# Retention outputs of one layer: PE's order set to transposes, preceding tile's outputs, gate products, scores, with q, k, v in a tile of their own

## The chip, the core and the metric

The kernel is one launch on one NeuronCore of a Trainium2 chip. The metric is the device time of that launch in microseconds (us), as the median of several runs. Five engines work beside each other, each through its own queue in order: PE (TensorE, the matrix engine), DVE (VectorE), ACT (ScalarE), POOL (GpSimd) and SP (SyncE, which here only issues DMAs).

## The reference

One layer of a hybrid backbone on 1024 tokens of width 1024 with 256 context tokens, in float32: modulated RMSNorm, one input projection, differential attention beside bidirectional retention, an output projection, then a routed mixture of 64 experts. The change lies in the retention, which in the reference reads (both directions; for a chunk of 128 tokens):

```
scores = einsum('bnihd,bnjhd->bnhij', qc, kc) * decay
intra  = einsum('bnhij,bnjhe->bnihe', scores, vc)
cross  = einsum('bnihd,nbhde->bnihe', q_dec, state_prev)
out    = intra + cross
r      = silu(gate) * rmsnorm(out, ret_norm_g)
```

Here `qc`, `kc` are 4 heads of 64, `vc` 4 heads of 128, `gate` is 512 columns of the input projection, and `state_prev` is the running sum of decayed k-v products that reaches the chunk.

## The kernel before, in words

The kernel runs stage after stage: column modulation, a projection of retention's q and k, the k-v products and states, **the retention outputs**, then queries, keys, values, attention, output projection, experts. Tiles are 128 tokens, so there are 8 of them, `t` = 0 to 7. A scheduler takes the program as written and puts each engine's instructions into a fixed order before the launch, by its own estimate of when each is ready; on the chip each engine then follows its list, waiting on semaphores. So the order of one engine can hold pieces of several tiles mixed, and a late instruction holds back everything behind it on its engine.

The retention outputs (lines 538 to 584) go through `t` from 7 down to 0. For one tile:

- `load_qkv` (L538) fetches q and k as `rqk` (L540) and v as `vt` (L542) from DRAM, where earlier stages stored them. It is called one tile ahead. Both tiles come from a ring of 10 buffers of 2 KB per partition, named `g2`, which all the small tiles of the stage share.
- `state_step` (L496 to L500) brings the backward state one tile further: DVE multiplies by the decay (`sst`, L499) and adds (`ST`, L500).
- `project` (L225) makes the gate: 24 products of 128x512 on PE (L228, tile `pp`: 8 slices of the width, each three times for a split of float32 in a high and a low part). ACT takes Silu of it (`gt`, L553) and POOL multiplies by the norm's weights (L554).
- PE transposes q and k (L555, recorded under the helper's line L392, `p<-cst,rqk`), and ACT copies them out (`qkT`, L557).
- DVE makes q with decay (`qd`, L559), PE transposes it (L561, again L392, `p<-cst,qd`), ACT copies it out (`qdT`, L563).
- PE makes the scores (`pss`, L567), DVE multiplies by the decay matrix `Dm` (`sT`, L569).
- PE makes the output (`po`): per head one product with v (L572) and one with the state (L573).
- ACT squares and sums the four heads (`sqs`, L577). `rstd_cols` (L154) takes the root: one operation on DVE (`rs_v`, L157) and one on POOL (`rs_r`, L159). DVE scales and gates the output (`r_o`, L581), SP stores it (L582).

Between these, `ada_rest` (L401) spreads other work over the stage: DMAs of 256 KB (`ada_l`, L408, two buffers) and one DVE operation on each (`ada_a`, L410 and L412); every eighth step, `ada_row` (L417) adds a product of one row on PE (`par`, L420) and a DVE operation on it (`ada_r`, L424 and L428). At the end of the stage `load_chunk` (L202) splits the next stage's weights: ACT makes the high part (`whi`, L209), DVE the low part (`wlo`, L210).

Of the kernel before, what the change touches and what calls it, by code (L numbers as in the profile page):

```python
# [9 lines left out]
F32 = mybir.dt.float32  # L10
# [4 lines left out]
AF = mybir.ActivationFunctionType  # L15
OP = mybir.AluOpType
# [4 lines left out]
P = 128  # L21
# [63 lines left out]
def hybrid_layer_kernel(ctx: ExitStack, tc: tile.TileContext, A, out, dbg=None):  # L85
    nc = tc.nc
    pe, dve, act, pool, sp = nc.tensor, nc.vector, nc.scalar, nc.gpsimd, nc.sync
# [90 lines left out]
    hv = ctx.enter_context(tc.tile_pool(name="hv", bufs=1, side="left"))  # L178
# [67 lines left out]
    NG2 = 10  # L246
# [9 lines left out]
    rng = wk.tile([P, P], F32, name="rng")  # L256
# [144 lines left out]
    def ada_rest(count):  # L401

        for n, k in ada_left[:count]:
            if k == 0:
                ada_acc[n] = wk.tile([P, 512], F32, name="ada_a", tag="ada_a", bufs=2)
            ac = ada_acc[n]
            aw = wk.tile([P, 512], F32, name="ada_l", tag="ada_l", bufs=2)
            sp.dma_start(aw, ada[:, k, 2048 + 512 * n:2560 + 512 * n])  # L408
            if k == 0:
                dve.tensor_scalar(ac, aw, cc[:, 0, 0:1], None, op0=OP.mult)  # L410
            else:
                dve.scalar_tensor_tensor(ac, aw, cc[:, k, 0:1], ac, op0=OP.mult, op1=OP.add)  # L412
            if k == 2 and n > 0:
                ada_row(n - 1)
        del ada_left[:count]

    def ada_row(n):  # L417
        c0 = 2048 + 512 * n
        pr_ = psa.tile([1, 512], F32, name="par", tag="po", bufs=2)
        pe.matmul(pr_, ones[:, 0:1], ada_acc.pop(n), start=True, stop=True)  # L420
        rw = wk.tile([1, 512], F32, name="ada_r", tag="ada_r")
        bw = wk.tile([1, 512], F32, name="ada_b", tag="ada_b")
        sp.dma_start(bw, A["ada_b"][:, c0:c0 + 512])
        dve.tensor_add(rw, pr_, bw)  # L424
        if n // 2 == 2:
            gw = wk.tile([1, 512], F32, name="ada_g", tag="ada_b")
            sp.dma_start(gw, A["norm2_g"][:, (n % 2) * 512:(n % 2 + 1) * 512])
            dve.scalar_tensor_tensor(rw, rw, 1.0, gw, op0=OP.add, op1=OP.mult)  # L428
        sp.dma_start(rows_d[n // 2:n // 2 + 1, (n % 2) * 512:(n % 2 + 1) * 512], rw)
# [5 lines left out]
    W = [], []  # L435
# [9 lines left out]
    for i, g in enumerate(pairs):  # L445
        for t in (2 * g - 2, 2 * g - 1):
            if t < 0:
                ps = project(t, W, 256, 512)
# [15 lines left out]
    Dm = wk.tile([P, H, P], F32, name="Dm")  # L464
# [26 lines left out]
    W = load_chunk(2048)  # L491
    ST = [s4.tile([P, 2, H, P], F32, name="ST") for _ in range(4)]
    ST = [ST[t // 2][:, t % 2] for t in range(NT)]
    GSb = GS[:, :, None].to_broadcast([P, H, P])

    def state_step(dst, src, kvp, half):  # L496
        s = slice(64 * half, 64 * half + 64)
        tmp = wk.tile([P, H, P], F32, name="sst", tag="g2", bufs=NG2)
        dve.tensor_tensor(tmp[s], src[s], GSb[s], op=OP.mult)  # L499
        dve.tensor_add(dst[s], tmp[s], kvp[s])  # L500

    kvc0 = None
    for t in range(-2, NT):
        ada_rest(VADA)
        ps = project(t, W)
# [13 lines left out]
        for h in range(H):  # L519
            pe.matmul(pk[:, h, :], kd[:, h].rearrange("p a b -> p (a b)"), v[:, h * P:(h + 1) * P],  # L520
                      start=True, stop=True)
# [13 lines left out]

    W = load_chunk(2560)

    def load_qkv(t):  # L538
        qk = wk.tile([P, 512], F32, name="rqk", tag="g2", bufs=NG2)
        sp.dma_start(qk, rqk_d[t * P:(t + 1) * P])  # L540
        vt = wk.tile([P, 512], F32, name="vt", tag="g2", bufs=NG2)
        sp.dma_start(vt, rv_d[t * P:(t + 1) * P])  # L542
        return qk, vt

    qkv = {NT - 1: load_qkv(NT - 1)}
    for t in reversed(range(NT)):
        qk, vt = qkv.pop(t)
        if t > 0:
            qkv[t - 1] = load_qkv(t - 1)
            state_step(ST[t - 1], ST[t], ST[t - 1], 1)  # L550
        ps = project(t, W)
        gt = wk.tile([P, H, P], F32, name="gt", tag="g2", bufs=NG2)
        act.activation(gt.rearrange("p h e -> p (h e)"), ps, AF.Silu)  # L553
        pool.tensor_tensor(gt, gt, rng[:, None, :].to_broadcast([P, H, P]), op=OP.mult)  # L554
        pt = transpose4(qk, "tp")  # L555
        qkT = wk.tile([P, 4, P], F32, name="qkT", tag="g2", bufs=NG2)
        act.activation(qkT, pt, AF.Copy)  # L557
        qd = wk.tile([P, H, 2, 64], F32, name="qd", tag="g2", bufs=NG2)
        dve.tensor_tensor(qd, qk[:, 0:256].rearrange("p (h d) -> p h d", h=H)[:, :, None, :].to_broadcast([P, H, 2, 64]),  # L559
                          Wd[:, 0, :, :, None].to_broadcast([P, H, 2, 64]), op=OP.mult)  # L560
        pt = transpose4(qd.rearrange("p h a d -> p (h a d)"), "tp")  # L561
        qdT = wk.tile([P, H, P], F32, name="qdT", tag="g2", bufs=NG2)
        act.activation(qdT, pt, AF.Copy)  # L563
        pss = psa.tile([P, 2, 4, P], F32, name="pss", tag="ps", bufs=1)
        for h in range(H):
            s = slice(64 * (h % 2), 64 * (h % 2) + 64)
            pe.matmul(pss[:, h % 2, h // 2, :], qkT[s, 2 + h // 2, :], qkT[s, h // 2, :], start=True, stop=True)  # L567
        sT = wk.tile([P, H, P], F32, name="sT", tag="g2", bufs=NG2)
        dve.tensor_tensor(sT.rearrange("p (a b) j -> p a b j", a=2), pss[:, :, 0:2, :], Dm.rearrange("p (a b) j -> p a b j", a=2), op=OP.mult)  # L569
        po_ = psa.tile([P, H, P], F32, name="po", tag="po", bufs=2)  # L570
        for h in range(H):
            pe.matmul(po_[:, h, :], sT[:, 2 * (h % 2) + h // 2, :], vt[:, h * P:(h + 1) * P], start=True, stop=False)  # L572
            pe.matmul(po_[:, h, :], qdT[:, h, :], ST[t][:, h, :], start=False, stop=True)  # L573
        ssq = wk.tile([P, 4], F32, name="ssq4", tag="ssq4", bufs=2)
        sqs = wk.tile([P, P], F32, name="sqs", tag="sqs", bufs=2)
        for h in range(H):
            act.activation(sqs, po_[:, h, :], AF.Square, accum_out=ssq[:, h:h + 1])  # L577
        rs = rstd_cols(wk, ssq, P, 4, 1.0 / P)
        r = wk.tile([P, H, P], F32, name="r_o", tag="g2", bufs=NG2)
        for h in range(H):  # L580
            dve.scalar_tensor_tensor(r[:, h, :], po_[:, h, :], rs[:, h:h + 1], gt[:, h, :], op0=OP.mult, op1=OP.mult)  # L581
        sp.dma_start(mix_d[t * P:(t + 1) * P, 512:1024], r.rearrange("p h e -> p (h e)"))  # L582
        ada_rest(GADA)
    ada_row(NT - 1)

    wk_ctx.close()
    NG2 = 4
    wq_ctx = ExitStack()
    wk = open_pool(wq_ctx, "wq", "right")
# [5 lines left out]
    W = load_chunk(0)  # L595
    for t in range(NT):
        o = apply_rope(wk, project(t, W), t, NG2)
        pt = transpose4(o, "tp")
        qs = wqs.tile([P, 4, 4, P], F32R, name="qs", tag="qs", bufs=2)
        for m in range(2):  # L600
            a, b = slice(64 * m, 64 * m + 64), slice(64 * (1 - m), 64 * (1 - m) + 64)
# [19 lines left out]
    W = load_chunk(512)  # L621
    for t in range(-2, NT):
        ps = project(t, W)
# [5 lines left out]
        pt = transpose4(o, "tp")  # L629
        c = slice((t + 2) * P, (t + 3) * P)  # L630
        for m in range(2):
            a, b = slice(64 * m, 64 * m + 64), slice(64 * (1 - m), 64 * (1 - m) + 64)
# [4 lines left out]
    W = load_chunk(1024)  # L637
# [20 lines left out]
    vt = [2 * g + j - 2 for g in (*LZ, 1, 4) for j in range(2)]  # L658
# [825 lines left out]
    with tc.For_i(0, n_over, 1) as j:  # L1484
        e = sp.value_load(olist[0:1, 0, bass.ds(j, 1)], min_val=0, max_val=NEXP - 1)
# [14 lines left out]
        for q in range(2):  # L1500
            pt = bank("tr", [P, 4, P])
# [5 lines left out]
        for i in range(2):  # L1507
            for k in range(KT):
                pe.matmul(pu[:, i * 256:(i + 1) * 256], xT[:, k, :], w13[:, i, k, :], start=(k == 0),
                          stop=(k == KT - 1))  # L1510
# [65 lines left out]
```

## Time and profile before

| what | value |
|---|---|
| median of 3 runs | 1822.42 us (1821.26 to 1834.03) |
| the profiled execution | 1815.02 us, its span 1813.2 us |
| mean granted TensorE clock | 0.968 of full |
| PE, DVE, ACT, POOL busy | 92%, 75%, 53%, 30% of the span |
| retention outputs | from about 180 to 284 us of the span |

The profile is of one execution. A row of a timeline gives the start, how long the instruction took, the engine, the line, what is written and read, and, in brackets, how long the engine had been idle before it and whose result it waited for. Durations of PE's products are modelled at their ends, so that neighbours overlap: spacing of starts says more than the duration. [...]

### The profile page before, as it was taken

The page shows a single profiled execution, that of the slowest core. Times are in us where ns is not written, and L with a number is a line of the kernel's source. Part 1 is how long each engine was busy: PE and PEld are TensorE (multiplying, and loading weights), DVE is VectorE, ACT ScalarE, POOL GpSimd, SP SyncE. Part 2 cuts the span into 40 slices and gives each one's busy share as a digit, 9 for nine tenths or more (in the row PEclk, how much of TensorE's full clock was granted, in tenths as well). Part 3 has the DMA queues.
Part 4 walks back from the last instruction along what each step waited for, and adds up shares of the span by engine and source line. Part 5 has one row for each costly group of instructions (what it writes and reads, how often), then busy time and mean ns, then how long its engine had stood idle before and what let it go on. Part 6 is the DMA issues. An engine that isn't in the chain of part 4 may idle for free.

```text
span 1813.2 us, 23071 instructions
## 1 busy us (share of the span) xinstructions
PE 1672.5 (92%) x8022; PEld 1273.8 (70%) x8022; DVE 1355.0 (75%) x2080; ACT 960.0 (53%) x1537; POOL 536.5 (30%) x384
## 2 busy tenths in 40 slices
PE   5899889999899989888899999999999999999992
PEld 3687667778666658666687777777777777777771
DVE  7866566651778766786577899888988989878873
ACT  6632223322578752232356787666765665566652
POOL 0100113200221130436434444343445343332331
PEclk9999989999899999998899999999999999999996
DMA  9675545801211144232989999999999999999976
GB/s 316 205 216 181 177 137 120 180 0 59 71 41 59 35 174 164 94 117 41 281 233 310 324 326 327 319 316 314 321 320 330 353 333 357 315 305 315 314 222 212
DMA packets 128413, 400.57 MB, mean 221 GB/s; under 512 B 13110, under 2 KB 49654, under 8 KB 103336
## 3 DMA queue, kind: packets, MB, share of 16 engines
q1 hardware_dynamic: 81000, 297.10, 45.8%
q0 software_dynamic: 46144, 97.80, 23.0%
q10 hardware_dynamic: 1152, 4.19, 0.6%
q8 instruction: 64, 1.05, 0.2%
q14 instruction: 53, 0.43, 0.1%
HBM read 324.45 MB, written 74.60 MB: 220 GB/s over the span
## 4 chain that ended last, share of the span: by engine, by line
PE 56%; DVE 15%; DMA 13%; ACT 7%; issue 5%; POOL 2%; another core or an unknown queue 1%; SPq 1%; POOLq 0%; ACTq 0%; DVEq 0%
PE up L1230 20%; PE py L1230 9%; PE pp L228 7%; DMA acc<-y,sidx 6%; PE tr L1214 3%; PE py L97 3%; PE pp L97 3%; DMA eraw<-in_exp_w_dram 3%; PE pS L97 3%; DVE w L1160 2%; ACT w L1159 2%; PE pu L97 2%; DVE nmx L729 2%; PE ptt L97 1%
## 5 line engine op out<-in xcount | busy, mean ns | idle before, releaser
L1230 PE MATMUL up<-w,xT 128*128 128x512 f32 (+1 forms) x2136 | 533.6, 399 | 4.7 <-DVE xT L1219 4.2
L1160 DVE TENSOR_TENSOR w<-eraw,w 128x1024 fp32r<-128x1024 f32 x390 | 459.8, 1217 | 43.3 <-ACT w L1159 41.9
L1159 ACT ACTIVATE w<-eraw 128x1024 fp32r<-128x1024 f32 x390 | 399.6, 1056 | 110.4 <-PE up L1230 59.1
L1230 PEld LDWEIGHTS up<-w,xT 128*128 128x128 f32 (+1 forms) x2136 | 384.5, 184 | 102.6 <-DVE xT L1219 7.8
L1169 POOL DMA_INDIRECT acc<-y,sidx x96 | 203.1, 2116 | 477.4 <-DMA acc<-y,sidx 215.6
L1230 PE MATMUL py<-w,ehT 128*128 128x512 f32 (+1 forms) x1116 | 293.6, 405 | 1.9 <-DVE ehT L1219 1.9
L1230 PEld LDWEIGHTS py<-w,ehT 128*128 128x128 f32 (+1 forms) x1116 | 198.2, 185 | 49.3 <-DVE ehT L1219 2.5
L1281 DVE SCALAR_TENSOR_TENSOR y<-py,swt,g2r 128x512 f32<-128x512 f32 (+2 forms) x192 | 137.9, 740 | 57.5 <-DMA acc<-y,sidx 38.7
L1198 POOL DMA_INDIRECT xg<-h2tab,sidx x96 | 132.8, 1384 | 68.5 <-PE tr L1214 43.6
L228 PE MATMUL pp<-whi,hTh 128*128 128x512 f32 (+1 forms) x368 | 148.0, 403 | 1.4 <-ACT hTh L386 1.2
L228 PE MATMUL pp<-wlo,hTh 128*128 128x512 f32 (+1 forms) x368 | 147.7, 403 | 0.0
L729 DVE TENSOR_REDUCE nmx<-pS 128x1 f32<-128x1280 f32 x64 | 95.1, 1487 | 67.2 <-PE pS L97 67.0
L1256 ACT ACTIVATE sl<-up 128x256 f32<-128x256 f32 (+1 forms) x104 | 39.7, 382 | 151.5 <-PE up L1230 139.9
L1219 DVE TENSOR_TENSOR xT<-tr,xT 128x512 fp32r<-128x512 f32 (+1 forms) x167 | 104.3, 655 | 14.9 <-ACT xT L1218 14.4
L159 POOL TENSOR_TENSOR rs_r<-rs_v,mhalf 128x1 f32<-128x1 f32 (+1 forms) x34 | 28.2, 830 | 268.3 <-DVE rs_v L157 166.7
L1018 POOL DMA_INDIRECT slots<-dat,ad x64 | 68.6, 1072 | 109.8 <-DVE dat L1015 54.9
L97 PE MATMUL pS<-K,qsl 128*128 128x512 f32 x336 | 94.7, 419 | 2.8 <-ACT an L737 1.9
L1258 DVE TENSOR_TENSOR hn<-up,sl 128x256 f32<-128x256 f32 (+1 forms) x104 | 64.8, 623 | 43.0 <-ACT sl L1256 42.0
L1218 ACT ACTIVATE xT<-tr 128x512 fp32r<-128x512 f32 (+1 forms) x167 | 89.1, 571 | 12.7 <-PE tr L1214 6.3
L1214 PEld LDWEIGHTS tr<-cst,xg 128*128 128x128 f32 (+2 forms) x800 | 79.0, 140 | 22.0 <-issue 7.1
L97 PE MATMUL py<-wo,mT 128*128 128x512 f32 x384 | 90.7, 393 | 0.0
L1214 PE MATMUL tr<-cst,xg 128*128 128x128 f32 (+2 forms) x800 | 90.3, 253 | 0.0
(324 smaller groups left out, 2503.7 us busy)
## 6 DMA issues: line engine op xcount, KB each, us to landing
eraw<-in_exp_w_dram SPq DMA_DIRECT2D x192, 1024.0 KB
ada_l<-in_ada_w_dram SPq DMA_DIRECT2D x64, 256.0 KB
wraw<-in_w_in_dram SPq DMA_DIRECT2D x24, 512.0 KB
aw<-in_ada_w_dram SPq DMA_DIRECT2D x8, 1024.0 KB
qsp<-qs POOLq DMA_DIRECT2D x32, 256.0 KB
qsl<-qsp POOLq DMA_DIRECT2D x7, 1024.0 KB
xt<-in_x_dram SPq DMA_DIRECT2D x8, 512.0 KB
wor<-in_w_out_dram SPq DMA_DIRECT2D x8, 512.0 KB
```

Of the source, the lines that this page charges most:

```text
L97: i = getattr(self.eng, name)(*args, **kw)
L228: pe.matmul(kw["out"], kw["lhsT"], kw["rhs"], start=kw["start"], stop=kw["stop"])
L729: dve.tensor_reduce(self.nmx, self.pS, axis=AX.X, op=OP.max, negate=True)
L1159: act.activation(hi, raw, AF.Copy)
L1160: dve.tensor_sub(lo, raw, hi.bitcast(F32))
L1169: x = pool.indirect_dma_start(out=acc, out_offset=bass.IndirectOffsetOnAxis(ap=idx, axis=0), in_=y, in_offset=None, compute_op=OP.add)
L1198: self.load = pool.indirect_dma_start(out=self.xg[:self.n], out_offset=None, in_=h2tab, in_offset=bass.IndirectOffsetOnAxis(ap=self.idx, a ...
L1214: pe.transpose(pt[:, i, :], src[:rows, k * P:(k + 1) * P], ident[:rows, :rows])
L1218: act.activation(hi, pt, AF.Copy)
L1219: dve.tensor_sub(lo, pt, hi.bitcast(F32))
L1230: pe.matmul(po, ops[o][:, k, :], w(k), start=(k == 0 and j == 0), stop=(k == nk - 1 and j == len(seq) - 1))
L1281: dve.scalar_tensor_tensor(y[:n, c], ps[i][:n], self.wt, g2r[:n, c], op0=OP.mult, op1=OP.mult)
```

## The change

The tile's work is written in another order, in a software pipeline of one tile. A tile's two sets of transposes come first, then the outputs of the preceding tile (`ret_out`, now a function), the state step and the loads for the next tile, the gate's products, the scores with `sT`. `qd` is now made in `load_qkv`, a tile ahead. q, k and v go into one tile `rows_qv` with two places (`t % 2`), in a buffer outside the ring (`hv0`, free in this stage). The last tile's outputs stand behind the loop. No arithmetic changes. (Numbers of lines below 544 move little; the lines of the kernel after are 9 higher from the next stage on.)

```diff
+    rows_qv = hv.tile([P, 2, 2, 512], F32, name="rows_qv", tag="hv0")
+
     def load_qkv(t):
-        qk = wk.tile([P, 512], F32, name="rqk", tag="g2", bufs=NG2)
+        qk, vt = rows_qv[:, t % 2, 0], rows_qv[:, t % 2, 1]
         sp.dma_start(qk, rqk_d[t * P:(t + 1) * P])
-        vt = wk.tile([P, 512], F32, name="vt", tag="g2", bufs=NG2)
         sp.dma_start(vt, rv_d[t * P:(t + 1) * P])
-        return qk, vt
+        qd = ...
+        dve.tensor_tensor(qd, ...)
+        return qk, vt, qd
+
+    def ret_out(t, sT, qdT, vt, gt):
+        ...
-    qkv = {NT - 1: load_qkv(NT - 1)}
-    for t in reversed(range(NT)):
-        ...
+    nxt, out_args = load_qkv(NT - 1), None
+    for t in reversed(range(NT)):
+        qk, vt, qd = nxt
+        pt = transpose4(qk, "tp")
+        ...
+        pt = transpose4(qd.rearrange("p h a d -> p (h a d)"), "tp")
+        ...
+        if out_args:
+            ret_out(*out_args)
+        if t > 0:
+            state_step(ST[t - 1], ST[t], ST[t - 1], 1)
+            nxt = load_qkv(t - 1)
+        ps = project(t, W)
+        ...
+        out_args = t, sT, qdT, vt, gt
         ada_rest(GADA)
+    ret_out(*out_args)
     ada_row(NT - 1)
```

PE before, around the outputs of tile 5 (`pss_1911`, `qd_1902` and `po_1918` are tile 5's, `pp_1978` is tile 4's gate; the number behind a name is the buffer's):

```order
L228 MATMUL pp_1978<-whi_1623,hTh3_674 128x512
L567 MATMUL pss_1911<-qkT_1900 128x128 x3
L392 MATMUL p4_1904<-cst_60,qd_1902 128x128 x4
L567 MATMUL pss_1911<-qkT_1900 128x128
L228 MATMUL pp_1978<-wlo_1624,hTh3_674 128x512
L228 MATMUL pp_1978<-whi_1623,hTlz_549 128x512
L228 MATMUL pp_1978<-whi_1629,hTh3_674 128x512
L228 MATMUL pp_1978<-wlo_1630,hTh3_674 128x512
L572 MATMUL po_1918<-vt_1760,sT_1916 128x128
```

Ahead of the outputs stand four products of the next tile's gate, behind the transposes of the tile's own `qd`. PE after, around the outputs of the same tile (`pss_1906`, `sT_1911` and `po_1955` are tile 5's, `p4_1941`, `qd_1876` and `pp_1987` tile 4's):

```order
L228 MATMUL pp_1878<-whi_1641,hTlz_549 128x512
L587 MATMUL pss_1906<-qkT_1837 128x128 x4
L420 MATMUL par_1916<-ada_a_1712,ones_63 1x512
L392 MATMUL p4_1941<-cst_60,rows_qv_1645 128x128 x4
L392 MATMUL p4_1948<-cst_60,qd_1876 128x128 x4
L554 MATMUL po_1955<-rows_qv_1645,sT_1911 128x128
```

Before, a tile's transposes of `qd`, its scores and its outputs stand a few gate products apart; after, the scores, the next tile's transposes and the outputs stand together, and 24 gate products in one piece follow.

DVE before, from the gating of tile 6 to the scores of tile 5:

```order
L157 TENSOR_SCALAR rs_v_1831<-ssq4_1825 128x4
L581 SCALAR_TENSOR_TENSOR r_o_1835<-po_1816,rs_r_1833,gt_1790 128x128 x4
L499 TENSOR_TENSOR sst_1864<-ST_1102,GS_138 64x512
L412 SCALAR_TENSOR_TENSOR ada_a_1853<-ada_l_1959,cc_99,ada_a_1853 128x512
L500 TENSOR_TENSOR ST_1102<-sst_1864,ST_1102 64x512
L559 TENSOR_TENSOR qd_1902<-rqk_1758,Wd_129 128x512
L412 SCALAR_TENSOR_TENSOR ada_a_1853<-ada_l_1962,cc_99,ada_a_1853 128x512
L569 TENSOR_TENSOR sT_1916<-pss_1911,Dm_1034 128x512
```

The tile's own `qd` and one `ada_a` stand ahead of its `sT`. DVE after, the same stretch (`qd_1876` is tile 4's):

```order
L157 TENSOR_SCALAR rs_v_1861<-ssq4_1855 128x4
L563 SCALAR_TENSOR_TENSOR r_o_1865<-po_1846,rs_r_1863,gt_1803 128x128 x4
L499 TENSOR_TENSOR sst_1871<-ST_1102,GS_138 64x512
L547 TENSOR_TENSOR qd_1876<-rows_qv_1645,Wd_129 128x512
L500 TENSOR_TENSOR ST_1102<-sst_1871,ST_1102 64x512
L412 SCALAR_TENSOR_TENSOR ada_a_1825<-ada_l_1935,cc_99,ada_a_1825 128x512
L412 SCALAR_TENSOR_TENSOR ada_a_1825<-ada_l_1938,cc_99,ada_a_1825 128x512
L589 TENSOR_TENSOR sT_1911<-pss_1906,Dm_1034 128x512
```

`qd` moved from the tile to the one ahead of it; the gating of tile 6 stands ahead of the scores of tile 5 in both.

## Rows read from the trace of the kernel before

**Rows 1.** The page's head and its first part: busy time, share of the span and instructions of each engine.

```profile
span 1813.2 us, 23071 instructions
PE 1672.5 (92%) x8022; PEld 1273.8 (70%) x8022; DVE 1355.0 (75%) x2080; ACT 960.0 (53%) x1537; POOL 536.5 (30%) x384
```

**Rows 2.** The view of windows: a stretch, its length, busy time of PE, of PE's weight loads, DVE, ACT and POOL with their counts, then the granted clock, the DMA share and GB/s.

```profile
175.00:190.00 15.00, 15.00 (x86) 12.31 (x85) 9.54 (x13) 6.75 (x9) 1.29 (x1) 1.00 0.91 307
190.00:205.00 15.00, 13.47 (x65) 10.12 (x65) 8.49 (x15) 4.62 (x19) 2.68 (x3) 0.89 0.49 149
220.00:235.00 15.00, 12.97 (x56) 9.80 (x55) 8.62 (x14) 3.16 (x11) 1.98 (x2) 0.77 0.36 114
280.00:295.00 15.00, 15.00 (x73) 11.72 (x72) 6.86 (x16) 3.83 (x13) 1.01 (x1) 1.00 0.05 19
...
188.15:190.13 1.98, 1.98 (x17) 1.86 (x16) 0.00 (x0) 0.00 (x0) 0.00 (x0) 1.00 0.92 347
228.85:232.28 3.43, 3.43 (x17) 3.31 (x15) 0.37 (x1) 0.00 (x0) 0.00 (x0) 0.53 0.52 153
258.29:260.07 1.78, 1.78 (x18) 1.78 (x16) 0.74 (x2) 0.00 (x0) 0.00 (x0) 1.00 0.56 157
...
188.15:280.70 92.55, 80.89 (x403) 62.54 (x403) 57.11 (x95) 25.97 (x81) 17.75 (x14) 0.89 0.47 148
```

**Rows 3.** The view of waits from 170 to 300 us: who waited for whom, us in total, times, the longest.

```profile
PE p L392 <- DVE qd L559: 11.7, 7, 2.3
```

**Rows 4.** The chain of work that ended last, in order of time: start, us, what.

```profile
143.32 5.36 PE pp L228 x23
...
183.35 0.44 PE p L392 x4
...
186.55 0.65 PE pss L567 x8
...
190.20 0.96 PE par L420 x2
...
192.18 1.09 POOL rs_r L159
```

**Rows 5.** The timeline of PE: start, us, engine, line, what, count, idle before.

```profile
163.85 1.13 PE L520 MATMUL pk<-rv,kd 128*128 128x128 f32 x8 [0.56 <-DVE kd L516]
...
188.15 0.49 PE L572 MATMUL po<-vt,sT 128*128 128x128 f32 x2
...
196.99 0.66 PE L392 MATMUL p<-cst,qd 128*128 128x128 f32 x4 [1.53 <-DVE qd L559]
...
210.77 0.66 PE L392 MATMUL p<-cst,qd 128*128 128x128 f32 x4 [2.28 <-DVE qd L559]
...
256.16 0.66 PE L392 MATMUL p<-cst,qd 128*128 128x128 f32 x4 [1.09 <-DVE qd L559]
...
280.70 0.38 PE L572 MATMUL po<-vt,sT 128*128 128x128 f32 x2
```

**Rows 6.** The timeline of DVE, columns as in rows 5.

```profile
175.61 2.35 DVE L210 TENSOR_TENSOR wlo<-wraw,whi 128x1024 fp32r<-128x1024 f32 x2
...
186.74 0.75 DVE L412 SCALAR_TENSOR_TENSOR ada_a<-ada_l,cc,ada_a 128x512 f32<-128x512 f32 x1 [3.07 <-DMA ada_l<-in_ada_w_dram]
187.41 0.68 DVE L569 TENSOR_TENSOR sT<-pss,Dm 128x512 f32<-128x512 f32 x1
...
194.46 1.75 DVE L499 TENSOR_TENSOR sst<-ST,GS 64x512 f32<-64x512 f32 x1
196.24 0.69 DVE L559 TENSOR_TENSOR qd<-rqk,Wd 128x512 f32<-128x512 f32 x1
196.97 0.69 DVE L500 TENSOR_TENSOR ST<-sst,ST 64x512 f32<-64x512 f32 x1
...
205.75 1.13 DVE L581 SCALAR_TENSOR_TENSOR r_o<-po,rs_r,gt 128x128 f32<-128x128 f32 x4 [1.19 <-POOL rs_r L159]
206.91 0.69 DVE L499 TENSOR_TENSOR sst<-ST,GS 64x512 f32<-64x512 f32 x1
207.63 1.65 DVE L412 SCALAR_TENSOR_TENSOR ada_a<-ada_l,cc,ada_a 128x512 f32<-128x512 f32 x1
...
277.40 1.13 DVE L581 SCALAR_TENSOR_TENSOR r_o<-po,rs_r,gt 128x128 f32<-128x128 f32 x4 [1.19 <-POOL rs_r L159]
```

**Rows 7.** The timelines of ACT and POOL, columns as in rows 5.

```profile
190.24 0.28 ACT L577 ACTIVATE sqs<-po 128x128 f32<-128x128 f32 x1 [3.06 <-PE po L573]
...
202.79 0.28 ACT L577 ACTIVATE sqs<-po 128x128 f32<-128x128 f32 x1 [4.46 <-PE po L573]
...
194.38 1.27 POOL L554 TENSOR_TENSOR gt<-gt,rng 128x512 f32<-128x512 f32 x1 [1.12 <-ACT gt L553]
...
207.19 1.53 POOL L554 TENSOR_TENSOR gt<-gt,rng 128x512 f32<-128x512 f32 x1 [1.48 <-ACT gt L553]
...
277.33 1.27 POOL L554 TENSOR_TENSOR gt<-gt,rng 128x512 f32<-128x512 f32 x1
```

More of the change, by code (lines that the diff above doesn't have):

```diff
@@ L536, in hybrid_layer_kernel @@
     W = load_chunk(2560)
+    rows_qv = hv.tile([P, 2, 2, 512], F32, name="rows_qv", tag="hv0")
     def load_qkv(t):
-        qk = wk.tile([P, 512], F32, name="rqk", tag="g2", bufs=NG2)
+        qk, vt = rows_qv[:, t % 2, 0], rows_qv[:, t % 2, 1]
         sp.dma_start(qk, rqk_d[t * P:(t + 1) * P])
-        vt = wk.tile([P, 512], F32, name="vt", tag="g2", bufs=NG2)
         sp.dma_start(vt, rv_d[t * P:(t + 1) * P])
-        return qk, vt
-    qkv = {NT - 1: load_qkv(NT - 1)}
-    for t in reversed(range(NT)):
[L547 to L557, printed above, removed]
         qd = wk.tile([P, H, 2, 64], F32, name="qd", tag="g2", bufs=NG2)
@@ L560, in hybrid_layer_kernel @@
                           Wd[:, 0, :, :, None].to_broadcast([P, H, 2, 64]), op=OP.mult)
[L561 to L569, printed above, removed]
+        return qk, vt, qd
+    def ret_out(t, sT, qdT, vt, gt):
         po_ = psa.tile([P, H, P], F32, name="po", tag="po", bufs=2)
@@ L582, in hybrid_layer_kernel @@
         sp.dma_start(mix_d[t * P:(t + 1) * P, 512:1024], r.rearrange("p h e -> p (h e)"))
+    nxt, out_args = load_qkv(NT - 1), None
+    for t in reversed(range(NT)):
+        qk, vt, qd = nxt
+        pt = transpose4(qk, "tp")
+        qkT = wk.tile([P, 4, P], F32, name="qkT", tag="g2", bufs=NG2)
+        act.activation(qkT, pt, AF.Copy)
+        pt = transpose4(qd.rearrange("p h a d -> p (h a d)"), "tp")
+        qdT = wk.tile([P, H, P], F32, name="qdT", tag="g2", bufs=NG2)
+        act.activation(qdT, pt, AF.Copy)
+        if out_args:
[4 more added lines that the diff above has]
+        ps = project(t, W)
+        gt = wk.tile([P, H, P], F32, name="gt", tag="g2", bufs=NG2)
+        act.activation(gt.rearrange("p h e -> p (h e)"), ps, AF.Silu)
+        pool.tensor_tensor(gt, gt, rng[:, None, :].to_broadcast([P, H, P]), op=OP.mult)
+        pss = psa.tile([P, 2, 4, P], F32, name="pss", tag="ps", bufs=1)
+        for h in range(H):
+            s = slice(64 * (h % 2), 64 * (h % 2) + 64)
+            pe.matmul(pss[:, h % 2, h // 2, :], qkT[s, 2 + h // 2, :], qkT[s, h // 2, :], start=True, stop=True)
+        sT = wk.tile([P, H, P], F32, name="sT", tag="g2", bufs=NG2)
+        dve.tensor_tensor(sT.rearrange("p (a b) j -> p a b j", a=2), pss[:, :, 0:2, :], Dm.rearrange("p (a b) j -> p a b j", a=2), op=OP.mult)
+        out_args = t, sT, qdT, vt, gt
         ada_rest(GADA)
+    ret_out(*out_args)
     ada_row(NT - 1)
```

## The prediction

> **What bounds the kernel now.** I read the page's busy shares first, then the windows over the stage, then who waited for whom, then the timelines of PE and DVE. PE is busy 92% of the span [rows 1], so a gain must come from places where it is not. The windows show one: from 175 to 190 us and from 280 to 295 PE is busy all the time at full clock, but between them it stands at 13.0 to 13.5 of 15 us, and the granted clock sinks to 0.77 in the worst stretch [rows 2]. That is the stage that is changed. From the first output of tile 7 at 188.15 to that of tile 0 at 280.70 there are seven gaps in 92.55 us, 13.2 us each [rows 2, 5].
>
> The waits name the reason: seven times PE waited for `qd`, 11.7 us together [rows 3]. [...]
>
> **What PE needs at least.** In the new order a gap holds 24 gate products at 5.36/23 = 0.233 us, so 5.6; scores 0.65; two sets of transposes at 0.44; outputs 1.98; together 9.1 us, and with `par` (0.96) 10.1 us, which stands in three of the seven gaps [rows 2, 4]. The transposes no longer wait: `qd` of a tile is made before the scores of the tile ahead of it, so the 11.7 us of waits on it go.
>
> **What is late next.** The change moves PE's list, but DVE's list keeps one thing: the gating `r_o` of a tile stands ahead of the scores `sT` of the next, and the outputs of the next tile need that `sT`. So a chain runs from output to output, through DVE, and I add it up:
>
> - outputs to the first square on ACT, 188.15 to 190.24: 2.09 [rows 5, 7]
> - first square to `r_o`, through ACT, DVE and POOL's root, 202.79 to 205.75: 2.96 [rows 6, 7]
> - `r_o` to `sst`, 205.75 to 206.91: 1.16; `sst` to the next, 0.72; `qd` 0.73; `ST` 0.72 like `sst` [rows 6]
> - two `ada_a` at a spacing of 0.67 (186.74 to 187.41): 1.34 [rows 6]
> - `sT` and the handover to PE, 187.41 to 188.15: 0.74 [rows 5, 6]
>
> The sum is 10.46 us. That is above PE's 9.1 and, by 0.4, above its 10.1. So PE will wait ahead of the outputs instead of ahead of the transposes of `qd`: shorter by some 3 us per gap than today's 13.2, if nothing is added. Two things are.
>
> First, POOL's `gt` follows the gate's products by ACT's Silu, and so falls beside `ST` and the two `ada_a`. Beside `gt`, `sst` took 1.75 instead of 0.69 us and an `ada_a` 1.65 instead of 0.75, and they ended only after POOL had; `r_o`, which reads `po` from PSUM, ran its 1.13 us beside `gt` unchanged [rows 6, 7]. I take 1.0 us per gap, between 0 (a `gt` that comes late meets nothing) and 1.06. What `gt` does to `sT`, no row shows; its operands are like those of `r_o` (one from PSUM), so I take 0, with the same bounds. [...]
>
> Second, a wait of 2 us or more ahead of the outputs brings the clock down, and the outputs are in the chain. They cost 1.45 more when all of them run at the lower level, 0 when the fall comes behind them. I take 0.5, near the 0 end, because in the gaps of before the lower level covered all of them only once [rows 2].
>
> **The sum.** A gap of 10.46 + 1.0 + 0.5 = 12.0 us. Five gaps (7 to 2) are like that: 60.0, plus 0.67 for an `ada_a` that the order puts into the `r_o` of tile 3: 60.7. The gap 2 to 1 has no `ada_a` left and `gt` meets only `sT`: 10.46 - 1.34 + 0.5 = 9.6. In the gap 1 to 0 the splits of the next weights, three `wlo`, stand between `r_o` and `sT`: 2.35 us for two [rows 6], so 3.5 for three; 2.09 + 2.96 + 1.16 + 3.5 + 0.74 + 1.0 + 0.5 = 12.0. Together 82.3, against 92.55: 10.2 us less.
>
> The ends: the `ada_a` ahead of tile 7's `sT` waited 3.07 us for its DMA [rows 6]. In SP's new order two of the four loads that stood ahead of that DMA are issued earlier. I take 1.0 us of gain, between 0 and the 3.07. Against that, the new PE order has 11 products fewer done when the last outputs begin (15 products of the queries' first tile stood ahead of the stage's last `par` before, 4 do now): 11 x 0.233 = 2.6 us to be done later. And behind the last outputs the clock is likely down, after the three `wlo`: 1.2 us, between 0 and 1.45. Behind the stage I count nothing: PE is busy all the time there [rows 2], so what is won is passed on, and the stages after are not touched.
>
> Net: 10.2 + 1.0 - 2.6 - 1.2 = 7.4 us. The profiled execution, 1813.2 us of span and 1.8 us around it, would take 1815.0 - 7.4 = 1807.6. The median of the runs, 1822.4, lies 7.4 us above that execution; the stage is the same in all, so I take the same us from it: 1822.4 - 7.4 = 1815.0 us, 0.4% less.
>
> **Edits that I cost at nothing.** The place for q, k, v outside the ring of ten: with two places, the load for tile t-2 must wait until tile t's outputs have read v. It stands in SP's queue ahead of the `ada_l` loads of the next gap, so these leave some 2.1 us into the gap and are wanted at 8.4 (2.09 + 2.96 + 1.16 + 0.72 + 0.73 + 0.72); 6.3 us of room cover twice the longest wait for such a load in the rows, 3.07 [rows 6]. If the cover is gone, a gap grows by what is late of it, since both `ada_a` stand in the chain. The store of `r_o`, too, holds SP; behind it stand only loads that are wanted after `sT`. ACT and POOL do the same work; ACT's evictions lie beside 24 gate products.
>
> **Rivals.**
>
> A. *The chain through DVE is not late, PE alone sets the gap.* For it: 24 products in one piece, and PE the busiest engine. Against it: the order, in which `sT` of a tile stands behind `r_o` of the tile before. Four gaps of 9.1 and three of 10.1 make 66.7, 25.9 less; 25.9 + 1.0 - 2.6 = 24.3 us: 1798 us.
>
> B. *The clock takes it all back, the kernel gets slower.* The wait now stands in one piece right ahead of the outputs, and the outputs are the first link of the chain. From a wait of 1.5 us on, the trace shows the fall. If it comes in every gap and covers the outputs, and the rest runs at the 0.77 of the stretch 220 to 235 [rows 2], the chain is 10.46 + 1.06 + 1.45 = 13.0 and PE's work 10.1/0.77 = 13.1: three gaps of 13.1, two of 13.0 with 0.67 more, 9.1/0.77 = 11.8 for the gap 2 to 1, and 13.0 make 90.8. That saves 1.8, and 2.6 + 1.45 go at the end: 2.3 us slower, 1824.7. Against it: after 1.09 us there was no fall, and gaps with `par` leave PE a wait of no more than 2 us. [...]
>
> C. *The loads are late* and the `ada_a` wait in each of the five gaps as the worst did, 3.07 us: 15 us given back on the forecast, 1830. Against it is the room worked out above.
>
> **How the numbers follow.** The forecast gets 0.64, A 0.12, B 0.19, C 0.05. The forecast's own bounds: with nothing added, five gaps of 10.46, 0.67, 9.1 and 10.45 make 72.5, so 20.0 + 3.1 - 2.6 = 20.5 gained, 1802; with everything added, five of 12.97, 0.67, 10.6 and 13.0 make 89.1, so 3.4 - 2.6 - 1.45 = 0.6 lost, 1823. The range, 1802 to 1825, takes in B and leaves out most of A and C. A measurement of this kernel can tell about 1% (18 us) from no change. Faster by more needs A or the forecast's very best end: 0.13. Slower by more than 18 us is none of the cases, and C with a bad draw comes nearest: 0.04. Within 1%: 0.83.
>
> **What would show it.** Right: no wait of PE for `qd`, but waits of 1 to 3 us ahead of the first output product of each tile, released by `sT`; gaps of about 12 us from output to output; `sst`, `ST` or `ada_a` of some 1.7 us beside `gt`; a stretch of lower clock in some of the gaps. Wrong: gaps of 9 to 10 us with PE busy throughout (A); 13 us and more with the outputs at 3.4 us in each (B); `ada_a` waiting for its DMA between `ST` and `sT` (C).

## The result and the profile after

The kernel after took 1810.34 us in the median of 15 runs, the kernel before 1821.26 us in 15 runs beside it: a ratio of 0.9941, 95% interval 0.9923 to 0.9960, or 10.7 us less (7.3 to 14.0). One of the 15 runs after took 3665.27 us and is not in the ratio. The forecast was 7.4 us less. The profiled execution took 1810.34 us, its span 1808.5. Executions of one kernel differ by more than the change (1809.7 to 1834.0 us for the kernel before), so where the time went is read from the stage and not from the spans.

The page of the kernel after, its head and busy times (before: [rows 1]):

```profile
span 1808.5 us, 23059 instructions
PE 1661.3 (92%) x8022; PEld 1264.4 (70%) x8022; DVE 1354.5 (75%) x2080; ACT 960.8 (53%) x1537; POOL 539.9 (30%) x384
```

The windows of the kernel after, columns as in [rows 2]. The fourth row goes from tile 7's first output to tile 0's, the last two are stretches at the lower clock:

```profile
190.00:205.00 15.00, 11.91 (x70) 10.09 (x69) 8.47 (x15) 3.39 (x13) 2.29 (x2) 0.92 0.56 177
220.00:235.00 15.00, 13.25 (x65) 10.40 (x64) 10.99 (x21) 3.15 (x11) 2.67 (x2) 0.89 0.46 148
280.00:295.00 15.00, 15.00 (x70) 12.06 (x69) 10.14 (x18) 4.74 (x8) 3.25 (x4) 1.00 0.41 71
...
189.25:270.81 81.56, 71.59 (x395) 56.17 (x395) 54.44 (x93) 24.16 (x78) 17.96 (x14) 0.96 0.45 145
202.47:205.84 3.37, 3.37 (x16) 3.08 (x15) 1.50 (x2) 1.02 (x6) 0.00 (x0) 0.50 0.69 210
226.13:229.88 3.75, 3.75 (x17) 3.71 (x18) 2.17 (x4) 0.12 (x1) 0.00 (x0) 0.54 0.70 228
```

The seven gaps took 81.56 us, against 92.55 in [rows 2]. Only two stretches at the lower clock (0.50 and 0.54) are left.

The waits from 170 to 300 us of the kernel after, columns as in [rows 3]. No row of PE waiting for `qd` is left; most of the wait has moved to `sT`, as forecast:

```profile
PE po L554 <- DVE sT L589: 10.5, 7, 3.1
DVE ada_a L412 <- DMA ada_l<-in_ada_w_dram: 16.2, 13, 2.8
```

The timeline of PE after, columns as in [rows 5]: the first output product of each tile, 7 to 0, and the one `par` that waited.

```profile
189.25 0.49 PE L554 MATMUL po<-rows_qv,sT 128*128 128x128 f32 x2 [1.35 <-DVE sT L589]
201.65 0.49 PE L554 MATMUL po<-rows_qv,sT 128*128 128x128 f32 x2 [3.09 <-DVE sT L589]
214.12 0.49 PE L554 MATMUL po<-rows_qv,sT 128*128 128x128 f32 x2 [0.60 <-DVE sT L589]
226.13 0.60 PE L554 MATMUL po<-rows_qv,sT 128*128 128x128 f32 x2 [1.75 <-DVE sT L589]
236.84 1.02 PE L420 MATMUL par<-ada_a,ones 128*1 128x512 f32 x2 [0.80 <-DVE ada_a L412]
238.85 0.49 PE L554 MATMUL po<-rows_qv,sT 128*128 128x128 f32 x2
251.46 0.49 PE L554 MATMUL po<-rows_qv,sT 128*128 128x128 f32 x2 [2.67 <-DVE sT L589]
260.57 0.49 PE L554 MATMUL po<-rows_qv,sT 128*128 128x128 f32 x2 [0.26 <-DVE sT L589]
270.81 0.49 PE L554 MATMUL po<-rows_qv,sT 128*128 128x128 f32 x2 [0.80 <-DVE sT L589]
```

The gaps are 12.40, 12.47, 12.01, 12.72, 12.61, 9.11 and 10.24 us. In the fourth (tile 4 to tile 3) the outputs waited for nothing: the wait stood two steps ahead of them, where `par` needs an `ada_a` of DVE, and the two sets of transposes follow `par`. A second profile of the same kernel has it longer:

```profile
234.52 1.02 PE L420 MATMUL par<-ada_a,ones 128*1 128x512 f32 x2 [2.21 <-DVE ada_a L412]
```

The timeline of DVE after in the first gap, and at its end one row of the last gap (before: [rows 6]):

```profile
192.99 0.75 DVE L412 SCALAR_TENSOR_TENSOR ada_a<-ada_l,cc,ada_a 128x512 f32<-128x512 f32 x1 [2.81 <-DMA ada_l<-in_ada_w_dram]
193.66 0.16 DVE L157 TENSOR_SCALAR rs_v<-ssq 128x4 f32<-128x4 f32 x1
195.01 1.13 DVE L563 SCALAR_TENSOR_TENSOR r_o<-po,rs_r,gt 128x128 f32<-128x128 f32 x4 [1.19 <-POOL rs_r L159]
196.17 0.69 DVE L499 TENSOR_TENSOR sst<-ST,GS 64x512 f32<-64x512 f32 x1
196.89 0.69 DVE L547 TENSOR_TENSOR qd<-rows_qv,Wd 128x512 f32<-128x512 f32 x1
197.62 1.81 DVE L500 TENSOR_TENSOR ST<-sst,ST 64x512 f32<-64x512 f32 x1
199.46 1.54 DVE L412 SCALAR_TENSOR_TENSOR ada_a<-ada_l,cc,ada_a 128x512 f32<-128x512 f32 x2
200.91 0.69 DVE L589 TENSOR_TENSOR sT<-pss,Dm 128x512 f32<-128x512 f32 x1
...
266.66 3.49 DVE L210 TENSOR_TENSOR wlo<-wraw,whi 128x1024 fp32r<-128x1024 f32 x3
```

The timelines of ACT and POOL after, in the first and the last gap (before: [rows 7]):

```profile
191.34 0.28 ACT L559 ACTIVATE sqs<-po 128x128 f32<-128x128 f32 x1 [2.70 <-PE po L555]
...
197.60 1.27 POOL L583 TENSOR_TENSOR gt<-gt,rng 128x512 f32<-128x512 f32 x1 [2.62 <-ACT gt L582]
...
268.93 2.34 POOL L583 TENSOR_TENSOR gt<-gt,rng 128x512 f32<-128x512 f32 x1 [3.35 <-ACT gt L582]
```

Read the first gap as the forecast's chain: outputs at 189.25, first square at 191.34 (2.09), `r_o` at 195.01 (3.67, since `rs_v` stood behind an `ada_a` that waited for its load), `sst` (1.16), `qd` (0.72), `ST` (0.73), which took 1.81 us beside `gt`, two `ada_a`, `sT` at 200.91, outputs at 201.65. No link is slack, and the sum is the gap: 12.40.

### The profile page after: what moved, and what is told of

It reads as the page before. It is cut to its first block, busy times and chain, and to the rows that moved or that the text cites. A ratio compares the mean times of both kernels' runs of the same rounds, so it can differ in the third digit from the quotient of the medians.

```text
span 1808.5 us, 23059 instructions
## 1 busy us (share of the span) xinstructions
PE 1661.3 (92%) x8022; PEld 1264.4 (70%) x8022; DVE 1354.5 (75%) x2080; ACT 960.8 (53%) x1537; POOL 539.9 (30%) x384
## 3 DMA queue, kind: packets, MB, share of 16 engines
q8 instruction: 64, 1.05, 0.2%
## 4 chain that ended last, share of the span: by engine, by line
PE 50%; DMA 18%; DVE 17%; ACT 7%; issue 5%; POOL 1%; SPq 1%; another core or an unknown queue 1%; POOLq 0%; DVEq 0%; ACTq 0%
PE up L1239 16%; DMA acc<-y,sidx 12%; PE py L1239 8%; PE pp L228 7%; PE py L97 3%; DVE w L1169 3%; PE pp L97 3%; PE tr L1223 3%; PE pS L97 3%; PE pu L97 2%; ACT w L1168 2%; DVE nmx L738 2%; DMA eraw<-in_exp_w_dram 1%; DMA ada_l<-in_ada_w_dram 1%; PE ptt L97 1%
## 5 line engine op out<-in xcount | busy, mean ns | idle before, releaser
L1168 ACT ACTIVATE w<-eraw 128x1024 fp32r<-128x1024 f32 x390 | 399.8, 1056 | 114.3 <-PE up L1239 60.7
L1239 PEld LDWEIGHTS up<-w,xT 128*128 128x128 f32 (+1 forms) x2136 | 382.7, 183 | 103.9 <-DVE xT L1228 10.2
L1178 POOL DMA_INDIRECT acc<-y,sidx x96 | 215.2, 2242 | 484.8 <-DMA acc<-y,sidx 158.9
L1207 POOL DMA_INDIRECT xg<-h2tab,sidx x96 | 122.3, 1274 | 64.2 <-PE tr L1223 40.6
```

What stands on the lines that cost most here:

```text
L1168: act.activation(hi, raw, AF.Copy)
L1178: x = pool.indirect_dma_start(out=acc, out_offset=bass.IndirectOffsetOnAxis(ap=idx, axis=0), in_=y, in_offset=None, compute_op=OP.add)
L1207: self.load = pool.indirect_dma_start(out=self.xg[:self.n], out_offset=None, in_=h2tab, in_offset=bass.IndirectOffsetOnAxis(ap=self.idx, a ...
L1239: pe.matmul(po, ops[o][:, k, :], w(k), start=(k == 0 and j == 0), stop=(k == nk - 1 and j == len(seq) - 1))
```

## The experiments

The seven gaps of a kernel are told as the distance from tile 7's first output product to tile 0's; a fall is a stretch at the lower clock between the two. For the whole stage I use the distance from the last state products `pk` to the third product of the queries' third tile (its first with `hTlz`), the same point in all kernels: 113.41 us in the profile of before (178.81 to 292.22), 105.25 in that of after (179.76 to 285.01).

**The state step ahead of the outputs.** Edit, in the kernel after:

```diff
+        if t > 0:
+            state_step(ST[t - 1], ST[t], ST[t - 1], 1)
         if out_args:
             ret_out(*out_args)
         if t > 0:
-            state_step(ST[t - 1], ST[t], ST[t - 1], 1)
             nxt = load_qkv(t - 1)
```

> The state step (sst and ST) is issued before the preceding tile's outputs instead of behind them; nothing else of the kernel after changes. DVE's list then has the state step in the wait for the squares, and between r_o and the next sT stand only qd and one or two ada_a. Theory (a chain through DVE sets the gap): 2.09 + 2.96 + 1.16 + 0.73 + 1.34 + 0.74 = 9.0 us, which is below what PE needs, so PE sets the gap: 9.5 us without par, 10.1 with it, and the seven gaps fall from 81.6 to about 69 us; the whole is some 12 us below the kernel after, ratio to before about 0.988; sT follows the scores at once, and PE's wait ahead of the outputs is 0.5 us or none. Rival 1 (the wait ahead of the outputs is not DVE's list but the distance from the scores to sT and back): the gaps stay at 12, ratio 0.994. Rival 2 (the DMAs of ada_l are behind): r_o waits behind an ada_a that waits for its load, gaps of 11 or more, ratio 0.992 to 0.994.

Measured: median 1781.61 us against 1803.72 of the kernel before on the same chip, ratio 0.9895 (0.9845 to 0.9944); gaps 69.80 us in all: 9.15, 11.42, 10.83, 10.10, 9.04, 9.09, 10.17. The windows, from first output to last:

```profile
189.07:258.87 69.80, 67.41 (x395) 53.17 (x395) 50.40 (x93) 24.37 (x79) 17.15 (x14) 1.00 0.52 163
```

The timeline of DVE in the first gap:

```profile
190.03 0.69 DVE L499 TENSOR_TENSOR sst<-ST,GS 64x512 f32<-64x512 f32 x1
190.75 0.69 DVE L500 TENSOR_TENSOR ST<-sst,ST 64x512 f32<-64x512 f32 x1
...
194.12 1.13 DVE L563 SCALAR_TENSOR_TENSOR r_o<-po,rs_r,gt 128x128 f32<-128x128 f32 x4 [1.20 <-POOL rs_r L159]
195.16 0.68 DVE L547 TENSOR_TENSOR qd<-rows_qv,Wd 128x512 f32<-128x512 f32 x1
195.76 1.53 DVE L412 SCALAR_TENSOR_TENSOR ada_a<-ada_l,cc,ada_a 128x512 f32<-128x512 f32 x2
197.41 0.69 DVE L590 TENSOR_TENSOR sT<-pss,Dm 128x512 f32<-128x512 f32 x1
```

The state step stands in DVE's idle time, PE is busy 67.41 of 69.80 us at full clock. The chain through DVE was what set the gaps: with 1.44 us taken out of it they fell almost to what PE needs, 66.7 us by the prediction's count. The five long gaps lost more than 1.44 each, 2.0 us against the mean of the four profiles of after (below): in three of them `gt` now came too late to hold up anything of the chain (at 197.42, 228.87 and 238.87; no instruction of the chain took more than 0.75 us beside it). The longest gap, 11.42, has something of the second rival in it, an `ada_a` ahead of `rs_v` that waits for its load:

```profile
203.50 0.75 DVE L412 SCALAR_TENSOR_TENSOR ada_a<-ada_l,cc,ada_a 128x512 f32<-128x512 f32 x1 [1.12 <-DMA ada_l<-in_ada_w_dram]
```

This version is faster than the kernel before. Against the kernel after its ratio alone does not decide (the interval reaches 0.9944, and after has 0.9941); the stage does, 92.67 us here against 102.3 to 105.3 in four profiles of after.

**No `gt` on POOL.** Edit, in the kernel after (the outputs lack the factor `rng`):

```diff
-        pool.tensor_tensor(gt, gt, rng[:, None, :].to_broadcast([P, H, P]), op=OP.mult)
```

> Leaves out POOL's multiplication of the gate gt by the norm weights rng, in the kernel after; the outputs lack that factor. Theory (gt holds up DVE's operations with two inputs in SBUF for about 1 us per gap, and these stand in the chain): the ST, ada_a that took 1.64 to 1.81 take 0.69 to 0.75, five gaps are shorter by 0.9 to 1.1 us each, and tile 7's first output comes 1.0 us earlier; the seven gaps fall from 81.6 to about 76.6, the whole is 5.9 us below the kernel after, ratio to before about 0.991. Rival (the slow instructions are beside the chain, or the wait is only moved): the gaps stay at 12.0 to 12.7 and the sum at 81 to 82, ratio 0.994.

Measured: gaps 76.33 us, the five long ones 11.86, 11.68, 11.01, 11.31, 11.12. The timeline of DVE in the first gap:

```profile
195.47 0.69 DVE L500 TENSOR_TENSOR ST<-sst,ST 64x512 f32<-64x512 f32 x1
196.19 1.54 DVE L412 SCALAR_TENSOR_TENSOR ada_a<-ada_l,cc,ada_a 128x512 f32<-128x512 f32 x2
197.65 0.68 DVE L588 TENSOR_TENSOR sT<-pss,Dm 128x512 f32<-128x512 f32 x1
```

`ST` took 0.69 us in place of 1.81. The five gaps are 5.2 us shorter in all than in the profile of after, as expected, though unevenly (0.5 to 1.5 us, with one fall of the clock here and two there). That profile is the longest of four of its kernel (below): against the four the five gaps are 2.9 to 5.2 us shorter, 3.8 in the mean. Tile 7's first output came 7.99 us after the last `pk`, 1.5 us sooner than in the profile of after and 1.0 sooner than in the mean of the four. (The whole took 2017 us. Without the factor the routing differs, and a loop at the program's end, which the kernel after does not enter, ran for some tokens; only the stage can be compared.)

**The room alone.** The kernel before with `qk` and `vt` in `rows_qv`:

```diff
+    rows_qv = hv.tile([P, 2, 2, 512], F32, name="rows_qv", tag="hv0")
-        qk = wk.tile([P, 512], F32, name="rqk", tag="g2", bufs=NG2)
-        vt = wk.tile([P, 512], F32, name="vt", tag="g2", bufs=NG2)
+        qk, vt = rows_qv[:, t % 2, 0], rows_qv[:, t % 2, 1]
```

> The kernel before with nothing changed but the place of q, k and v: rows_qv with two places instead of buffers of the ring. Theory (the gain comes from the order, the room is worth nothing by itself): the seven gaps add up to 92 to 93 us as before, PE waits seven times for qd, 11 to 12 us together, ratio to before 1.000. Rival (buffers of the ring held up the loads and with them qd): the waits for qd shrink, the gaps add up to 82 to 87 us, ratio 0.994 to 0.997.

Measured: ratio 0.9976 (0.9948 to 1.0003); waits for `qd` 10.5 us; gaps 85.74 us, with two falls where before has five. That is neither of the two: the waits hardly shrank, the gaps did. Once more, with the kernels of the next runs:

> The room alone once more (q, k and v of the kernel before in rows_qv, nothing else). Theory 1 (the clock's falls make most of its 6.8 us): the sum of the gaps differs from 85.7 by a few us, between 85 and 92, ratio 0.997 to 1.000. Theory 2 (the room makes it): 85 to 86.5 us and two falls again, ratio 0.995 to 0.997.

Measured: ratio 1.0004 (0.9975 to 1.0033), gaps 85.95 us, waits 10.7 us, two falls. The gaps and the falls are those of theory 2, the ratio is nearer to that of theory 1. The stage (106.17 and 106.36 us) is shorter than that of before; the whole shows no gain that can be told from none.

**The order alone.** The kernel after with q, k and v in the ring:

```diff
-    rows_qv = hv.tile([P, 2, 2, 512], F32, name="rows_qv", tag="hv0")
-        qk, vt = rows_qv[:, t % 2, 0], rows_qv[:, t % 2, 1]
+        qk = wk.tile([P, 512], F32, name="rqk", tag="g2", bufs=NG2)
+        vt = wk.tile([P, 512], F32, name="vt", tag="g2", bufs=NG2)
```

> The kernel after with nothing changed but the place of q, k and v: in the ring of ten, as before the change. DVE's list has qd last ahead of sT then, but the same instructions between r_o and sT. Theory (the order alone makes the gain, and the same chain through DVE bounds it): the seven gaps add up to 81 to 83 us, ratio to before 0.993 to 0.996; part of PE's wait stands ahead of the transposes of qd, up to 2 us of each, and less ahead of the outputs, the sum of both unchanged. Rival (the room is what lets the loads come early enough): qd waits for rqk, the gaps add up to 85 to 92 us, ratio 0.997 to 1.000.

Measured: ratio 0.9967 (0.9941 to 0.9994), gaps 82.43 us, three falls. Its waits from 170 to 300 us:

```profile
PE p L392 <- DVE qd L547: 8.5, 5, 2.6
PE p L392 <- DMA rqk<-rqk_d: 2.5, 3, 1.3
DVE qd L547 <- DMA rqk<-rqk_d: 1.1, 2, 0.7
PE po L554 <- DVE sT L589: 0.8, 1, 0.8
```

The five long gaps take 61.9 us, about as long as in the kernel after (60.8 in the mean), and PE's wait merely stands ahead of the transposes of `qd` again. The late loads of `rqk` (3.6 us of waits) are what the room saves; the gaps are 0.9 us longer than in the profile of after (1.6 longer than the mean of its four), and the stage takes 106.49 us against 105.25 (104.0 in the mean).

**How often the clock falls.** Both kernels unchanged, three more profiles each.

> The kernel before, unchanged, once more with a profile. Its seven gaps were 92.6 us with four or five falls of the clock, and those of the kernel with the room alone 85.7 us with two; PE's waits for qd were 11.7 and 10.5 us. Theory 1 (the room is worth about 1 us, and the rest of the difference is how often the clock fell, which changes from execution to execution): the sum comes out anywhere between 86 and 93 us, with fewer than four falls where it is short. Theory 2 (the room itself makes the difference): 92 to 93 us and four or five falls again.

> The kernel after, unchanged, on the same chip as the other kernels of this group. The seven gaps again 81 to 83 us, since the chain through DVE sets them whether the clock falls or not (each fall that covers the outputs costs up to 1.45 us); which gaps see a fall may change. Ratio to before 0.992 to 0.996.

> The kernel before, unchanged, a third profile. So far its two profiles show five and four falls of the clock between the first and the last outputs, with the same seven waits for qd (11.7 us). Theory 1 (the falls belong to the order of before: they come in most executions): four or five again, the gaps 89 to 93 us. Theory 2 (the falls come and go by execution alike in both kernels): any number from none to five, the gaps 82 to 93 us.

> The kernel after, unchanged, a third profile. So far two falls (81.6 us) and none (79.4 us), with waits of 10.5 and 9.7 us ahead of the outputs. Theory 1 (the falls belong to the order): none to two again, 79 to 82 us. Theory 2 (they come and go alike): up to five, 79 to 87 us.

> The kernel before, unchanged, a fourth profile. Theory 1: four or five falls, the gaps 89 to 93 us. Theory 2: none to five, 82 to 93 us.

> The kernel after, unchanged, a fourth profile. Theory 1: none to two falls, 79 to 82 us. Theory 2: up to five, 79 to 87 us.

Measured: the windows from first output to last. The kernel before, second profile:

```profile
189.89:279.43 89.54, 77.88 (x402) 60.36 (x402) 57.07 (x95) 25.98 (x81) 17.74 (x14) 0.92 0.48 151
```

The kernel before, third profile:

```profile
189.48:277.32 87.84, 76.14 (x403) 58.62 (x403) 57.03 (x95) 26.01 (x81) 17.78 (x14) 0.94 0.49 154
```

The kernel before, fourth profile:

```profile
188.12:277.53 89.41, 77.79 (x402) 60.24 (x402) 57.02 (x95) 25.98 (x81) 17.73 (x14) 0.92 0.48 151
```

The kernel after, second profile:

```profile
188.80:268.21 79.41, 68.11 (x394) 53.06 (x394) 54.46 (x93) 24.30 (x79) 17.57 (x14) 1.00 0.46 145
```

The kernel after, third profile:

```profile
189.70:271.12 81.42, 71.88 (x395) 56.86 (x395) 53.66 (x93) 24.26 (x79) 17.45 (x14) 0.94 0.45 143
```

The kernel after, fourth profile:

```profile
187.97:268.77 80.80, 71.44 (x394) 56.24 (x394) 54.27 (x93) 24.10 (x78) 17.99 (x14) 0.96 0.45 146
```

The granted clock (third number from the end) and PE's busy time are what to read. Falls, counted with the first profiles: 5, 4, 3, 4 before; 2, 0, 2, 2 after. The second profile of before, 89.54 us, speaks against the 92 to 93 of its theory 2, and the second of after, 79.41 us, came out below the 81 to 83 that I had expected. For the last four, theory 1 (the falls belong to the order) holds apart from the 3 (and 87.84 us) of one profile: the old order has more of them, but how many changes from execution to execution. The second run of after was also timed: ratio 0.9943 (0.9913 to 0.9973).

Put together, the mean sum of the gaps went from 89.8 to 80.8 us. PE's idle time in them (length less PE busy) went from 11.7 to 10.0, only 1.6 less. PE's busy time went from 78.2 to 70.8, 7.4 less: 2.6 are the products moved behind the last outputs, 1.0 a `par` that now stands ahead of the first, and the remaining 3.8 fit the granted clock, 0.92 in the mean before and 0.965 after (0.08 of 89.8 us less 0.035 of 80.8 would be 4.4, with PE busy throughout). The stage as a whole went from 110.7 to 104.0 us in the mean, 6.7 less: 3.8 from the clock, 1.6 from shorter waits, and 1.3 ahead of tile 7's first output (0.3, and the `par` that it now has to wait for). So one wait was mostly exchanged for another, and by this account over half of the gain in the stage came through the clock. It is an account: no run changes the clock alone.

**The state step and `qd` ahead of the outputs.** As the first experiment, with q's load split off and moved too:

```diff
             state_step(ST[t - 1], ST[t], ST[t - 1], 1)
+            nxt = load_qkv(t - 1)
         if out_args:
             ret_out(*out_args)
         if t > 0:
-            nxt = load_qkv(t - 1)
+            vt_n = load_v(t - 1)
```

> As the run with the state step ahead of the preceding outputs, and q's load and qd moved there too; v's load stays behind. Between r_o and the next sT stand only one or two ada_a. Theory (PE sets the gap now): nothing more to win where the gap was 9.1 or 10.1; the two gaps that were 11.42 and 10.83 lose up to 0.7 us each; the sum 68 to 70 us, ratio within 0.001 of that run, 0.988 to 0.991. Rival (DVE's chain still counts): another 0.7 us in each of six gaps, 65.6 us.

Measured: ratio 0.9876 (0.9836 to 0.9917), beside 0.9943 of the kernel after in the same group; gaps 69.26 us at full clock. Another 0.7 us taken out of DVE's chain gave 0.5 us in all: for the most part PE sets the gaps there. Tile 7's first output came 1.0 us later after the last `pk` than in the first experiment (9.65 against 8.65 us), so that the stage, 93.10 us, is no shorter than its 92.67.

## Why the prediction was right, point by point

- **The waits for `qd` go, a chain through DVE is next: right.** The row is gone, and in the profile of after `sT` releases the outputs of seven tiles of eight. The five long gaps were forecast at 60.7 us and took 62.21, 60.07, 61.01 and 59.83 in the four profiles. The links themselves show best in the gap 2 to 1, where no `ada_a` stands in the chain and `gt` met only `sT`: without a fall it took 9.11 us, and 10.46 - 1.34 is 9.12. Taking 1.44 us out of the chain took most of the wait away: 2.5 us of waits for `sT` were left of 10.5.
- **`gt`, 1.0 us per gap, nothing on `sT`: right.** In 19 of the 20 long gaps of the four profiles one instruction took 0.7 to 1.1 us more beside `gt`. Without `gt` the gaps lost 3.8 us in the mean, 0.8 a gap, and not all of that 1.0: in the first of them an `ada_a` ahead of `rs_v` then waited longer for its load, which gave back 0.6 of the first profile's gap. Beside `gt` (197.42 to 198.69 in the first experiment) `sT` took its 0.69 us, from 197.41. `ST`, whose two inputs both lie in SBUF, took 1.81 us beside `gt` in the profile of after.
- **The gap 1 to 0, forecast 12.0, was 10.24: mis-sized.** The 1.0 us for `gt` did not come. The three `wlo` ran their 1.16 us each, and it was `gt` that took 2.34. It came at 268.93, while a `wlo` was running; in the first gap `ST` came at 197.62, just behind `gt` at 197.60, and there it was `ST` that took longer (1.81 us, `gt` 1.27). I had not asked who came first.
- **The clock, 0.5 per gap in the chain: too much, by about half.** The profile of after without a fall has 60.07 us in the five gaps, the three with falls 61.0 in the mean: about 0.2 a gap. Two things had no term and fill part of the difference. The loads of `ada_l` cost 0.7 us in the first gap, ahead of `rs_v` and not ahead of `sT`. And in the gap 4 to 3 `par` waits for an `ada_a`: the forecast had `par` only in what PE needs, not in the chain. In the second profile the outputs there came 1.61 us after the start of `sT` (234.79 to 236.40), in place of 0.74. That a wait of 2 us or more, or one from 1.5 us on, brings the clock down was my reading of two waits, 1.53 and 2.28 us [rows 5]; no run shows such a threshold. The trace of before has a fall after 1.33 us (last section), and in the kernel after a wait of 2.67 us passed without one. The 1.45 us for outputs wholly at the lower clock are 3.43 less 1.98 [rows 2].
- **The 1.2 us of low clock behind the last outputs: wrong, 0.** From tile 0's first output to the queries' third tile it is 14.20 us, 14.19 to 14.21 in the other three, at a granted clock of 1.00 in the first, against 11.52 before: 2.7 more, which is the 2.6 of the 11 products alone.
- **Tile 7 1.0 us earlier: mis-sized, 0.3.** From the last `pk` to its first output: 9.36 in the mean of four before, 9.02 after. The wait of 3.07 us for a load is gone or shorter, but a `par` and `gt` now stand in its place: without `gt` it was 7.99.
- **Where it is measured from.** [rows 2] shows 92.55 us, the longest of four; the mean is 89.8. That I had not allowed for. Against it the forecast sum of 82.3 (80.8 measured) is worth 7.5 and not 10.2. With the clock's 1.2 not lost, the net is 6.7 in the stage, beside the forecast of 7.4. That it is closer than its terms is luck: 2.7 us too much from the baseline and 0.7 from tile 7 stand against 1.5 by which the gaps were shorter than forecast and 1.2 of clock that were not lost.
- **The room "costed at nothing": not quite.** Alone it shortened the gaps by 4 us against the mean of before, with waits for `qd` only 1.1 us shorter and two falls, and the whole shows nothing of it; with the order it saves the late loads of `rqk`.
- **The rivals.** A did not hold: gaps of 12, not 9 to 10, with the PE bound nearly reached only once the state step had moved. B did not hold: none to two falls after, and the time did not come back. In the profile of after the waits of PE were 0.3 to 3.1 us, and the clock fell after those of 3.09 and 1.75 us (granted 0.50 and 0.54); in the second profile it fell after none. C did not hold where it was put: no `ada_a` between `ST` and `sT` waited for its load. Elsewhere they did wait, 16.2 us in all over 13 times, mostly in DVE's idle time.

Left open: why the clock fell more often in the old order (3 to 5 times against 0 to 2) at waits of about the same length (11.7 and 10.0 us in all), why the room alone has fewer falls, and what the difference between 6.7 us in the stage and 10.7 in the whole is. The 6.7 lie just below the measured interval (7.3 to 14.0); the spans of the four profiles of each kernel differ by 7.8 in the mean, inside it, so that about 1 us of these lies outside the stage. Open is also how much of the gain is the order's and how much the room's: each alone shortened the stage by some 4 us, both together by 6.7.

## What to carry to other kernels

When a change removes a wait, write down every engine's list between two repeats of the same work, add up the chain that is left, and only then ask what PE needs: here the scores of a tile stood behind the gating of the tile before, and independent work (the state step) stood between them while DVE idled earlier. Moving that work into the idle time was worth another 11 us in the stage, more than the change itself. And take the baseline of a stage from more than one profile: it differed by 4.7 us between executions of one kernel.

## What the runs showed of the hardware

The same wait is not always followed by a fall. In the kernel before, PE waits 1.33 us for tile 3's `qd`. The timeline of PE in the profile of before, where the next products are 0.43 us apart:

```profile
240.57 0.65 PE L392 MATMUL p<-cst,qd 128*128 128x128 f32 x4 [1.33 <-DVE qd L559]
...
242.79 0.63 PE L228 MATMUL pp<-whi,hTlz 128*128 128x512 f32 x1
243.22 0.63 PE L228 MATMUL pp<-whi,hTh 128*128 128x512 f32 x1
```

And in its second profile, where they are 0.23 apart:

```profile
240.85 0.66 PE L392 MATMUL p<-cst,qd 128*128 128x128 f32 x4 [1.33 <-DVE qd L559]
...
242.87 0.39 PE L228 MATMUL pp<-whi,hTlz 128*128 128x512 f32 x1
243.10 0.39 PE L228 MATMUL pp<-whi,hTh 128*128 128x512 f32 x1
```

The gap in which this wait stands took 15.65 us in the first and 13.62 in the second. Not all of that is this fall: 1.05 us of the 2.0 lie at the gap's start, where tile 4's outputs ran longer under an earlier fall (3.43 us against 2.38). A cleaner price comes from the second and third profiles of before, whose falls differ by one alone, after the wait of 1.52 us for tile 6's `qd`: the two gaps that it touches took 25.11 us with it and 23.64 without, 1.5 us for one fall.

In the kernel after a wait of 2.62 to 2.67 us ahead of tile 2's outputs was followed by no fall in two of the four profiles and by one in the other two. In the two kernels whose waits were no longer than 1.51 us (the first and the last experiment, one profile each) no fall shows in the stage: the granted clock is 1.00 from the first output to the last.
